# A fourth buffer for split weights, an early start of the state space stage's weights, and an early load of the square root's table

## The chip, the cores and the metric

The kernel runs on one core of a Trainium2 chip. The metric is the device time of one execution in microseconds (us), taken as the median of several executions. Engines are named as in the profile: PE multiplies matrices (TensorE), PEld loads its weights, DVE is VectorE, ACT is ScalarE, POOL is GpSimd, and SP issues most of the loads from memory.

## The reference, cut to what matters

One decoder layer is computed for 576 tokens, 512 of a prompt and 8 sequences of 8 sample tokens, with model width 1024, in float32:

```python
h = modulate(x, g_pre[0], shift0, scale0)
x = x + 0.5 * gate0 * rms_norm(swiglu(h, w_gate[0], w_up[0], w_down[0]), g_post[0])     # width 2816
h = modulate(x, g_pre[1], shift1, scale1)
q_lat, kv_lat, k_rope, z, xBC, dt, g_attn, g_ssm = split(h @ w_in)
o_attn = mla_attention(q_lat, kv_lat, k_rope) @ w_o_attn       # prompt, and samples over a paged cache
o_ssm  = mamba2(z, causal_conv(xBC), dt, state) @ w_o_ssm      # 4 groups of 8 heads, chunks of 128
mixed  = (sigmoid(g_attn) * o_attn + sigmoid(g_ssm) * o_ssm) @ w_out
x = x + gate1 * rms_norm(mixed, g_post[1])
h = modulate(x, g_pre[2], shift2, scale2)
x = x + 0.5 * gate2 * rms_norm(swiglu(h, w_gate[1], w_up[1], w_down[1]), g_post[2])
```

`rms_norm` divides by a root of the mean square; `modulate` is a norm with a scale and a shift from the sequence's vector. Outputs are x, the latent cache rows, and the new convolution and state space states.

## The kernel before, in words

Channels lie on the 128 partitions and tokens along the free dimension, in two halves of 288 tokens (`HALF`). Nearly every product is made three times in a reduced float32 format: each operand is split in a high part, `hi`, and a remainder, `lo`, and PE sums hi by hi, hi by lo and lo by hi. Activations are split where they are made. Weights are split when they arrive: `weights` (line 146) loads a 512 KB tile `wraw` on SP's queue, ACT copies it to `whi` (line 167), and DVE, or POOL for every second tile once `pool_weights` is set, subtracts to give `wlo` (line 113, called from line 168). The count that picks the engine, `wcount`, goes up by one with every call of `weights`. The pool `wp` holds three buffers each of `wraw`, `whi` and `wlo`. A pool `up` of 40 equal buffers of 608 floats per partition (`NU`) holds nearly everything else: activations, convolution rows, chunk matrices, states.

`gemm` splits a tile's weights and puts its product on a list, `pending`; a product is issued when more than `look[0]` are on that list. One tile of 8 by 128 input channels is 24 matmuls for one token half and 48 for both. `product` also runs the closures left on `later` after its matmuls and before its own evacuation. `flush` issues everything that is pending.

`Split` computes half 0 of all its tiles first, then half 1, so that the second half's input may come late. The split weights of its last `keep` tiles stay in `whi` and `wlo` for the second half, those of `far` more tiles stay in buffers of `up` (four of them for a tile), and the rest are loaded and split again.

The stages in order of time: the first feed-forward block, whose hidden width beyond the first six tiles goes through a seven-product block scheme (class `Wino`, lines 213 to 293: seven small weight blocks for each pair of tiles, two blocks in one `whi` buffer); its last down projection, merged with the normalisation of half 0 (`renew`); the first eleven tiles of `w_in` in a `Split` named `few` (gates, six convolution tiles of state space group 0, and the tile with dt); the state space stage; the latent and key/query tiles; attention of the prompt; attention of the samples; the two output projections; the second feed-forward block, which begins with another `Split`.

Outside of a block `with in_order():` a planner orders the instructions of each engine by its own estimate of times. Inside, PE, ACT, DVE and POOL run in the order in which the program is written. The state space stage is such a block: a generator `dense` issues the projections, a generator `scan` the chunks, and lines 1366 to 1378 interleave them. Before its first chunk the block calls `next(work)` `PRE` = 4 times, which splits four tiles of group 1 and issues two products. Ahead of it, lines 1005 to 1010 run the second half of `few`, call the three steps of `steps()` (time steps, sums, and a small product at line 979 that needs `last` from DVE at line 976), and `flush`.

`Sums` adds squares over tiles: `add` squares a tile on ACT (line 440), accumulates on POOL or DVE, and after the last tile a product with ones (line 430) sums over partitions. `rnorm` (line 451) takes the root on ACT and the reciprocal on DVE. The root needs another table of ACT than Silu, Tanh and Exp, and the compiler puts a table load ahead of the instruction that needs it.

Of the kernel before, what the change touches and what calls it, by code (L numbers as in the profile page):

```python
# [9 lines left out]
F32R = mybir.dt.float32r  # L10
BF16 = mybir.dt.bfloat16
I32 = mybir.dt.int32
AF = mybir.ActivationFunctionType
# [9 lines left out]
SCALE = 96 ** -0.5  # L23
NEG = -3.0e38
GAP = 603
NU = 40


def layer_kernel(tc, A, O, tap=None, stop=None):
# [7 lines left out]
def _layer(ctx, tc, A, O, tap, stop):  # L37
    nc = tc.nc
    V, S, PE, G = nc.vector, nc.scalar, nc.tensor, nc.gpsimd

    cp = ctx.enter_context(tc.tile_pool(name="cp", bufs=1))
    up = ctx.enter_context(tc.tile_pool(name="up", bufs=NU))
    wp = ctx.enter_context(tc.tile_pool(name="wp", bufs=3))
# [51 lines left out]
    def small(shape, dt=F32):  # L95
        return sp.tile(shape, dt, tag="small", name="small", bufs=24)
# [12 lines left out]
    def f32(ap):  # L109
        return ap.bitcast(F32)  # L110
# [18 lines left out]
    def in_order():  # L129

        E = mybir.EngineType
        return tc.manual_schedule(engines={E.PE, E.Activation, E.DVE, E.Pool})
# [15 lines left out]
    def weights(src, kc, far=False):  # L148

        out = []  # L150
        wcount[0] += 1
        pool = wcount[0] % 2 == 0 and pool_weights[0]
        for k0 in range(0, kc, 8):
            n = min(8, kc - k0)
            raw = wp.tile([128, 8, 128], F32, tag="wraw", name="wraw")
            if far:
                load(raw[:, :n], src[:, k0 * 128:(k0 + n) * 128].rearrange("p (k m) -> p k m", m=128))
                for k in range(0, n, 4):
                    hi, lo = (utile(F32R, [128, 4, 128], t) for t in ("fhi", "flo"))
                    S.copy(hi, raw[:, k:k + 4])  # L160
                    sub(lo, raw[:, k:k + 4], f32(hi), pool)
                    out += [(hi[:, j], lo[:, j]) for j in range(4)]
                continue
            hi = wp.tile([128, 8, 128], F32R, tag="whi", name="whi")
            lo = wp.tile([128, 8, 128], F32R, tag="wlo", name="wlo")
            load(raw[:, :n], src[:, k0 * 128:(k0 + n) * 128].rearrange("p (k m) -> p k m", m=128))
            S.copy(hi[:, :n], raw[:, :n])  # L167
            sub(lo[:, :n], raw[:, :n], f32(hi[:, :n]), pool)
            out += [(hi[:, j], lo[:, j]) for j in range(n)]
        return out  # L170
# [10 lines left out]
    look = [0]  # L181
# [33 lines left out]
    def flush():  # L215
        while pending:
            pending.pop(0)()
        settle()

    class Wino:  # L220
# [3 lines left out]
        def __init__(self, kc, x, area):  # L224

            self.kc, self.x, self.area, self.store = kc, x, area, None

        def block(self, src):

            kc = self.kc  # L230
            if self.store is None:
                self.store = [wp.tile([128, 2, 4, 128], F32R, tag=t, name=t) for t in ("whi", "wlo")]
                n = 0
            else:
                n = 1
            hi, lo = (t[:, n, :kc] for t in self.store)
            if n == 1:
                self.store = None
            S.copy(hi, src)  # L239
            sub(lo, src, f32(hi))  # L240
            return [(hi[:, j], lo[:, j]) for j in range(kc)]
# [56 lines left out]
    class Split:  # L298

        def __init__(self, tiles, kc, xh, xl, first=0, keep=2, then=None, far=0):
            self.tiles, self.kc, self.xh, self.xl, self.first, self.keep, self.then = tiles, kc, xh, xl, first, keep, then
            self.far = far

        def half0(self, first=True, last=True):
            if first:
                flush()
            kc, xh, xl, few = self.kc, self.xh, self.xl, self.first
            self.w = w = [weights(src, kc) for src, _ in self.tiles[:few]]  # L310
            if self.then:
                self.then()
            if few:
                ps = [mmt() for _ in range(few)]
                for k in range(kc):
                    for n in range(few):
                        mm3(ps[n][:, :HALF], *w[n][k], xh(k, 0), xl(k, 0), k == 0, k == kc - 1)
                for n in range(few):
                    self.tiles[n][1](0, 0, ps[n][:, :HALF])
            n0 = len(self.tiles) - self.keep  # L320
            for n, (src, evac) in enumerate(self.tiles[few:], few):
                w.append(weights(src, kc, n0 - self.far <= n < n0))
                gemm(None, kc, xh, xl, evac, (0,), w=w[-1])
                yield
            if last:
                flush()
# [92 lines left out]
    class Sums:  # L419
# [12 lines left out]
        def add(self, src, wait=False):  # L432
            self.k += 1
            last = self.k == self.n
            if self.acc is None:
                self.acc = s = utile(F32, [128, HALF], "acc")
                S.activation(s, src, AF.Square)
            else:
                s = tmp("sq")
                S.activation(s, src, AF.Square)  # L440
                (G if self.pool and not last else V).tensor_tensor(self.acc, self.acc, s, ALU.add)  # L441
            if last or self.k % self.group == 0:
                acc, self.acc = self.acc, None
                if wait:
                    later.append(lambda: self.square(acc, last))
                else:
                    self.square(acc, last)
# [143 lines left out]
    def ffn(n, xh, xl, side, last, wino, first=0, again=None):  # L591
# [39 lines left out]
        for part, (a, b) in enumerate(PARTS):  # L631
# [3 lines left out]
            tiles = []  # L635
# [36 lines left out]
            if part == 0:  # L672
                if again:
                    few = Split(tiles, 8, *parts(lambda k: (xhs[:, k], xls[:, k])), first, then=again[0])
                    yield few.half0()
                    merge((few.half1(), 1), (again[1], AGAIN))
                else:
                    few = Split(tiles, 8, *X, first)
# [12 lines left out]
            H = parts(lambda k, hs=hs: hs[k])  # L691
# [14 lines left out]
            tiles = [(A["w_dn"][n, m, :, 128 * a:128 * b], ev_down(m)) for m in range(NQ)]  # L706
            if part < end_:
                for src, ev in tiles:
                    if part:
                        product(src, b - a, *H, ev)  # L710
                    else:
                        gemm(src, b - a, *H, ev)
                        next(sums_, None)
            else:
                run(side)
                down = Split(tiles, b - a, *H, far=3)
                half0 = down.half0(first=False)
                next(half0)
                pending.insert(-1, settle)
                next(half0)  # L720
                wino.end()
                run(half0)
                merge((down.half1(), 1), (last(0, f, sums[0]), RENEW))
                yield last(1, f, sums[1])
# [9 lines left out]
    xT, _ = xtile(F32, "xT")  # L734
# [74 lines left out]
    xh, xl = X2s  # L809
# [184 lines left out]
    few = Split([gate(m) for m in next_gates(EARLY)] + c0[:5] + [(W[2], ev_kd), c0[5]], 8, *X2)  # L994
# [7 lines left out]
    done("x1")  # L1002
    pool_weights[0] = True
    st = steps()
    for n, _ in enumerate(few.half1()):
        if n in (2, 7):
            next(st, None)
    run(st)
    look[0] = 0
    flush()  # L1010

    def chunk_fetch(it):
        g, c = it["g"], it["c"]
# [281 lines left out]
    osm, _ = xtile(F32, "osm")  # L1295
# [15 lines left out]
    PRE = 4  # L1311
# [51 lines left out]
    work = dense()  # L1363
    age = 0
    credit = 1.0
    with in_order():
        look[0] = 2
        for _ in range(PRE):
            next(work)
        for _ in scan():  # L1370
            if kept:
                age += 1
                if age > 1:
                    put()
                    age = 0
            credit += RATE[min(len(closed), 3)]
            while credit >= 1:
                next(work, None)
                credit -= 1
        run(work)  # L1380
        flush()
        put()
        look[0] = 0
# [8 lines left out]
    for m in range(NQ):  # L1392
        ts = utile(F32, [128, T], "ts")
        load(ts, gscr[8 + m])
        for i in range(2):
            c = slice(i * HALF, i * HALF + HALF)
# [25 lines left out]
    def value_weights(p):  # L1422
        raw = wp.tile([128, 2, 256], F32, tag="wraw", name="wraw")
        if p == 0:
            wh, wl = (wp.tile([128, 2, 256], F32R, tag=t, name="wv") for t in ("whi", "wlo"))
        else:
            wh, wl = (vwp.tile([128, 2, 256], F32R, tag="wv", name="wv") for _ in range(2))
        load(raw, A["w_uv"][p // 2].rearrange("p (k b) -> p k b", k=2))
        S.copy(wh, raw)
        G.tensor_tensor(wl, raw, f32(wh), ALU.subtract)  # L1430
        wv_[p // 2] = wh, wl
# [352 lines left out]

    def split(it):

        it["c"] = hi, lo = [wp.tile([128, 4, 256], F32R, tag=t, name="c" + t) for t in ("whi", "wlo")]
        it["kp"] = kp = utile(F32R, [96, 4, 128], "kp")
        S.copy(hi[:, :, :128], it["raw"][:, :, 256:384])
        S.copy(kp, it["raw"][:96, :, 512:])  # L1790
# [167 lines left out]
    wv = []  # L1958
# [51 lines left out]
    xT, _ = xtile(F32, "xT2")  # L2010
# [169 lines left out]
```

## Time and profile before

| | us |
|---|---|
| median of 3 runs | 1990.33 (1987.17 to 1992.01) |
| the profiled execution | 1989.74 |
| its span, first to last instruction | 1988.0 |
| PE / DVE / ACT / POOL busy | 1889.4 / 1426.6 / 1023.5 / 628.2 |

The mean granted clock of PE in the span is 0.985 of full speed. The page gives 1368 matmuls of each of the three kinds for line 203's `xh`/`xl` products alone, at about 300 ns of overlapping duration each. In the rows below a `[x <-...]` at the end of a line is the time for which the engine sat idle before the instruction and what ended that.

### The profile page before, as it was taken

Reading aid. Unit: us, or ns where it says so; the run is one execution under the profiler, and the core shown is the slowest. Engines: PE = TensorE matmul, PEld = TensorE weight load, DVE = VectorE, ACT = ScalarE, POOL = GpSimd, SP = SyncE. Lnnn points to the kernel's source line nnn. Section 1 sums busy time; section 2 is a strip of 40 time slices with the busy share of each in tenths; the row PEclk is TensorE's granted clock in tenths of the full one; section 3 lists DMA queues with packets and bytes.
Section 4 is the critical chain, followed back from the end, with each engine's and each line's share of the span. In section 5 each row is a group of like instructions: output and inputs, shape, how many; then the busy total and the mean of one; then the engine's idle time right before and its main releaser. Section 6 shows DMA issues by size and latency. Waiting matters only on the chain.

```text
span 1988.0 us, 37032 instructions
## 1 busy us (share of the span) xinstructions
PE 1889.4 (95%) x13779; PEld 1746.5 (88%) x13779; DVE 1426.6 (72%) x2595; ACT 1023.5 (51%) x2237; POOL 628.2 (32%) x645
## 2 busy tenths in 40 slices
PE   6999999998989999999999899999989999999997
PEld 5999888998888999999899778776688999999997
DVE  4787575868776685667767677788956884866885
ACT  4655343556555465545434456566545664534553
POOL 1214234416343232332333111133332421422533
PEclk9999999999989999999999999999999999999998
DMA  9433545354554538454536444287857553232252
GB/s 322 138 117 122 188 136 170 98 172 131 183 130 147 160 105 221 127 177 149 165 108 210 136 165 138 89 272 265 288 181 244 164 171 99 83 97 87 94 168 77
DMA packets 171670, 312.79 MB, mean 157 GB/s; under 512 B 18097, under 2 KB 84370, under 8 KB 171490
## 3 DMA queue, kind: packets, MB, share of 16 engines
q1 hardware_dynamic: 145506, 267.93, 42.4%
q0 software_dynamic: 9088, 34.11, 4.9%
q10 hardware_dynamic: 16896, 8.39, 1.5%
q8 instruction: 108, 1.77, 0.4%
q14 instruction: 72, 0.59, 0.1%
HBM read 283.54 MB, written 26.83 MB: 156 GB/s over the span
## 4 chain that ended last, share of the span: by engine, by line
PE 44%; DVE 10%; ACT 3%; DMA 3%; issue 2%; POOL 1%; SPq 0%; DVEq 0%; ACTq 0%; POOLq 0%
PE mm L203 27%; PE mm L264 5%; DVE wlo L113 2%; PE mm L1576 2%; DMA wraw<-w_gu 1%; PE aux L1852 1%; DVE kp L113 1%; PE aux L1649 1%; DVE xbc L849 1%; PE mm L174 1%; ACT whi L167 1%; POOL cwlo L113 1%; PE mm L1631 1%; DVE small L1825 1%; PE mm L175 1%
## 5 line engine op out<-in xcount | busy, mean ns | idle before, releaser
L113 DVE TENSOR_TENSOR wlo<-wraw,whi 128x512 fp32r<-128x512 f32 (+2 forms) x296 | 320.9, 1086 | 126.9 <-ACT whi L167 86.5
L167 ACT CAST whi<-wraw 128x1024 fp32r<-128x1024 f32 (+2 forms) x260 | 234.2, 902 | 254.2 <-PE mm L203 146.1
L203 PE MATMUL mm<-xh,whi 128*128 128x288 f32 (+1 forms) x1368 | 346.2, 303 | 7.9 <-ACT xh L492 4.4
L203 PE MATMUL mm<-xl,whi 128*128 128x288 f32 (+1 forms) x1368 | 342.0, 300 | 4.1 <-DVE xl L482 3.2
L203 PE MATMUL mm<-xh,wlo 128*128 128x288 f32 (+1 forms) x1368 | 339.2, 298 | 6.6 <-POOL wlo L113 6.5
L203 PEld LDWEIGHTS mm<-xh,whi 128*128 128x128 f32 x1368 | 238.5, 192 | 16.0 <-ACT xh L492 4.6
L203 PEld LDWEIGHTS mm<-xh,wlo 128*128 128x128 f32 x1368 | 238.1, 191 | 7.6 <-POOL wlo L113 6.9
L203 PEld LDWEIGHTS mm<-xl,whi 128*128 128x128 f32 x1368 | 238.3, 191 | 5.7 <-DVE xl L482 3.9
L113 POOL TENSOR_TENSOR wlo<-wraw,whi 128x1024 fp32r<-128x1024 f32 (+1 forms) x60 | 122.6, 2044 | 166.4 <-ACT whi L167 159.3
L264 PE MATMUL mm<-t,whi 128*128 128x288 f32 x768 | 154.4, 295 | 1.3 <-DVE u L289 0.9
L264 PE MATMUL mm<-xh,wlo 128*128 128x288 f32 x512 | 150.1, 297 | 1.8 <-DVE wlo L113 1.8
L203 PE MATMUL mm<-hl,whi 128*128 128x288 f32 x608 | 151.5, 295 | 0.0
L264 PE MATMUL mm<-xl,whi 128*128 128x288 f32 x512 | 151.5, 297 | 0.0
L203 PE MATMUL mm<-hh,whi 128*128 128x288 f32 x608 | 151.2, 295 | 0.0
L264 PE MATMUL mm<-xh,whi 128*128 128x288 f32 x512 | 149.7, 297 | 0.0
L203 PE MATMUL mm<-hh,wlo 128*128 128x288 f32 x608 | 148.7, 296 | 0.3 <-DVE wlo L113 0.3
L113 DVE TENSOR_TENSOR wlo<-area,whi 128x512 fp32r<-128x512 f32 x128 | 116.4, 931 | 14.0 <-ACT whi L239 12.8
L264 PEld LDWEIGHTS mm<-t,whi 128*128 128x128 f32 x768 | 123.0, 188 | 3.2 <-issue 1.3
L264 PE MATMUL mm<-t,wlo 128*128 128x288 f32 x384 | 113.0, 296 | 1.7 <-DVE wlo L113 1.7
L441 POOL TENSOR_TENSOR acc<-acc,sq 128x288 f32<-128x288 f32 x72 | 71.5, 995 | 126.3 <-ACT sq L440 102.4
L203 PEld LDWEIGHTS mm<-hl,whi 128*128 128x128 f32 x608 | 104.9, 188 | 3.4 <-issue 3.4
L203 PEld LDWEIGHTS mm<-hh,whi 128*128 128x128 f32 x608 | 104.7, 188 | 3.5 <-ACT whi L167 1.7
(440 smaller groups left out, 4685.0 us busy)
## 6 DMA issues: line engine op xcount, KB each, us to landing
wraw<-w_gu SPq DMA_DIRECT2D x108, 512.0 KB, 3.5
craw<-cache SPq DMA_DIRECT2D x128, 320.0 KB, 4.4
wraw<-w_in SPq DMA_DIRECT2D x72, 512.0 KB, 4.0
wada<-w_ada SPq DMA_DIRECT2D x80, 256.0 KB, 4.6
area<-w_ada POOLq DMA_DIRECT2D x16, 1024.0 KB, 6.0
wraw<-w_dn SPq DMA_DIRECT2D x22, 512.0 KB, 4.7
wraw<-w_dn SPq DMA_DIRECT2D x32, 256.0 KB, 2.7
M<-cscr SPq DMA_DIRECT2D x32, 256.0 KB, 5.1
```

Of the source, the lines that this page charges most:

```text
L113: (G if pool else V).tensor_tensor(out, a, b, ALU.subtract)
L167: S.copy(hi[:, :n], raw[:, :n])
L174: PE.matmul(ps, ah, bl, start=False, stop=False, skip_group_check=skip)
L175: PE.matmul(ps, al, bh, start=False, stop=stop, skip_group_check=skip)
L203: PE.matmul(p[:, :m.shape[-1]], a, m, start=(k == 0 and n == 0), stop=(k == kc - 1 and n == 2))
L264: PE.matmul(ps, l, r, start=(start and j == 0 and n == 0), stop=(stop and j == self.kc - 1 and n == 2), skip_group_check=True)
L441: (G if self.pool and not last else V).tensor_tensor(self.acc, self.acc, s, ALU.add)
L849: V.scalar_tensor_tensor(a[:, 0:600], u[:, k:k + 600], cw[:, n, k:k + 1], a[:, 0:600], ALU.mult, ALU.add)
L1576: PE.matmul(pss[i][:, :HALF], a, x[k][:, i * HALF:i * HALF + HALF], start=(k == 0 and a is w[k][0] and x is qlh), stop=(k == 3 and a is w[ ...
L1631: PE.transpose(ps[:, c0 + 128 * (i - j):c0 + 128 * (i - j) + 128], block(p, e, i, j), ident)
L1649: PE.matmul(ps[64 * e:64 * e + 64, 128 * j:TP], vt[j // 2][:, j % 2, c0:c0 + 64], src, start=(j == 0), stop=(j == 3), tile_position=(0, 64 ...
L1825: V.tensor_reduce(mx[:, g:g + 1], ps, AX.X, ALU.max)
```

## The change

Four buffers of `whi` and `wlo` where there were three; `NU` goes from 40 to 37. The last down projection of each feed-forward block keeps two far tiles where it kept three. `few.half1` no longer flushes, and the flush after the steps is gone; two of the four calls of `next(work)` now come ahead of the ordered block. After the square of the last but one tile of a sum with `wait`, ACT takes the root of one column into a small tile that nobody reads. `Split` takes a parameter `spare`, which no caller passes.

```diff
-NU = 40
+NU = 37
@@ weights (also Wino.block, value_weights and the samples' split)
-            hi = wp.tile([128, 8, 128], F32R, tag="whi", name="whi")
-            lo = wp.tile([128, 8, 128], F32R, tag="wlo", name="wlo")
+            hi = wp.tile([128, 8, 128], F32R, tag="whi", name="whi", bufs=4)
+            lo = wp.tile([128, 8, 128], F32R, tag="wlo", name="wlo", bufs=4)
@@ Split.half0
-                w.append(weights(src, kc, n0 - self.far <= n < n0))
+                w.append(weights(src, kc, n0 - self.far <= n < n0 or n in self.spare))
@@ Sums.add
+            if wait and self.k == self.n - 1:
+                S.activation(small([128, 1]), s[:, 0:1], AF.Sqrt)
@@ ffn, last part
-                down = Split(tiles, b - a, *H, far=3)
+                down = Split(tiles, b - a, *H, far=2)
@@ second half of few
-    for n, _ in enumerate(few.half1()):
+    for n, _ in enumerate(few.half1(False)):
         if n in (2, 7):
             next(st, None)
     run(st)
-    look[0] = 0
-    flush()
@@ state space stage
+    look[0] = 2
+    for _ in range(2):
+        next(work)
     with in_order():
-        look[0] = 2
-        for _ in range(PRE):
+        for _ in range(PRE - 2):
             next(work)
```

## Rows read from the trace of the kernel before

**Rows 1.** The page's part 1: busy us, share of the span, instructions.
```profile
PE 1889.4 (95%) x13779; PEld 1746.5 (88%) x13779; DVE 1426.6 (72%) x2595; ACT 1023.5 (51%) x2237; POOL 628.2 (32%) x645
```
**Rows 2.** Busy time by stretch: PE, PEld, DVE, ACT, POOL, granted clock, DMA share, GB/s.
```profile
550.00:575.00 25.00, 18.11 (x115) 17.69 (x114) 17.68 (x19) 10.16 (x19) 11.97 (x17) 0.80 0.48 127
1650.00:1675.00 25.00, 25.00 (x190) 25.00 (x189) 12.99 (x25) 11.23 (x26) 0.98 (x1) 1.00 0.34 99
```
**Rows 3.** Waits of PE in the whole span: total us, times, longest.
```profile
PE mm L203 <- POOL wlo L113: 7.7, 3, 5.2
...
PE mm L203 <- ACT whi L167: 4.0, 5, 2.1
...
PE mm L264 <- DVE wlo L113: 3.5, 5, 1.4
...
PE mm L203 <- DVE wlo L113: 2.7, 4, 1.8
```
**Rows 4.** PE's timeline, 554.5 to 563 us: start, duration, instruction, idle before.
```profile
556.63 0.48 PE L979 MATMUL aux<-last,psel 32*128 32x128 f32 x2 [1.65 <-DVE last L976]
562.36 0.85 PE L203 MATMUL mm<-xh,wlo 128*128 128x288 f32 x2 [5.24 <-POOL wlo L113]
```
**Rows 5.** POOL's timeline, 555 to 567 us.
```profile
556.27 3.01 POOL L846 COPY ncvs<-u 128x24 f32<-128x24 f32 x1
...
559.43 2.87 POOL L113 TENSOR_TENSOR wlo<-wraw,whi 128x1024 fp32r<-128x1024 f32 x1
```
**Rows 6.** ACT's timeline, 547 to 571 us.
```profile
547.99 1.05 ACT L167 CAST whi<-wraw 128x1024 fp32r<-128x1024 f32 x1 [0.36 <-PE mm L203]
...
570.98 0.40 ACT L836 COPY u<-mm 128x288 f32<-128x288 f32 x1 [6.46 <-PE mm L203]
```
**Rows 7.** Busy time by stretch around the entry of the state space stage.
```profile
555.00:562.00 7.00, 0.48 (x2) 0.29 (x2) 6.96 (x8) 2.71 (x6) 6.21 (x5) 0.71 0.48 126
562.00:567.00 5.00, 4.64 (x19) 4.65 (x20) 3.88 (x3) 0.70 (x1) 4.09 (x6) 0.50 0.46 138
```
**Rows 8.** DVE's timeline, 441 to 470 and 555 to 573 us.
```profile
444.86 1.97 DVE L452 RECIPROCAL aux<-aux 128x288 f32<-128x288 f32 x1 [1.28 <-ACT aux L451]
...
556.50 1.21 DVE L113 TENSOR_TENSOR wlo<-wraw,whi 128x1024 fp32r<-128x1024 f32 x1
...
572.77 0.84 DVE L849 SCALAR_TENSOR_TENSOR xbc<-u,conv_w,xbc 128x600 f32<-128x600 f32 x1 [6.03 <-ACT xbc L847]
```
**Rows 9.** PE's timeline at three more waits.
```profile
469.19 1.09 PE L203 MATMUL mm<-xh,whi 128*128 128x288 f32 x3 [4.36 <-ACT xh L492]
...
1521.89 0.41 PE L203 MATMUL mm<-ahl,wlo 128*128 128x288 f32 x1 [1.82 <-DVE wlo L113]
...
1581.29 0.41 PE L203 MATMUL mm<-xh,whi 128*128 128x288 f32 x1 [2.12 <-ACT whi L167]
```
**Rows 10.** Busy time by stretch after the wait at 1581 us.
```profile
1582.00:1585.40 3.40, 3.40 (x16) 3.40 (x15) 3.40 (x5) 1.27 (x4) 1.54 (x2) 0.50 0.70 233
```
**Rows 11.** ACT's timeline around roots, and around the wait at 1581 us.
```profile
443.06 1.28 ACT L451 ACT_TABLE_LOAD   x1
444.35 0.47 ACT L451 ACTIVATE aux<-aux,eps_t 128x288 f32<-128x288 f32 x1
...
1514.39 0.47 ACT L451 ACTIVATE aux<-aux,eps_t 128x288 f32<-128x288 f32 x1 [1.37 <-PE aux L430]
...
1577.53 1.05 ACT L167 CAST whi<-wraw 128x1024 fp32r<-128x1024 f32 x1 [1.10 <-PE mm L203]
1578.60 1.28 ACT L642 ACT_TABLE_LOAD   x1
```
**Rows 12.** Waits in the state space stage, 575 to 1040 us: of SP, ACT, PE.
```profile
SPq L63 <- DMA o_ssm_s<-sn: 43.7, 11, 16.9
...
ACT whi L167 <- DMA o_ssm_s<-sn: 27.2, 3, 13.2
...
PE aux L1059 <- DVE H L1113: 3.1, 4, 1.9
```

More of the change, by code (lines that the diff above doesn't have):

```diff
@@ L231, in block @@
             if self.store is None:
-                self.store = [wp.tile([128, 2, 4, 128], F32R, tag=t, name=t) for t in ("whi", "wlo")]
+                self.store = [wp.tile([128, 2, 4, 128], F32R, tag=t, name=t, bufs=4) for t in ("whi", "wlo")]
                 n = 0
@@ L298, in _layer, with __init__ @@
     class Split:
-        def __init__(self, tiles, kc, xh, xl, first=0, keep=2, then=None, far=0):
+        def __init__(self, tiles, kc, xh, xl, first=0, keep=2, then=None, far=0, spare=()):
             self.tiles, self.kc, self.xh, self.xl, self.first, self.keep, self.then = tiles, kc, xh, xl, first, keep, then
-            self.far = far
+            self.far, self.spare = far, spare
         def half0(self, first=True, last=True):
@@ L1424, in value_weights @@
         if p == 0:
-            wh, wl = (wp.tile([128, 2, 256], F32R, tag=t, name="wv") for t in ("whi", "wlo"))
+            wh, wl = (wp.tile([128, 2, 256], F32R, tag=t, name="wv", bufs=4) for t in ("whi", "wlo"))
         else:
@@ L1785, in split @@
     def split(it):
-        it["c"] = hi, lo = [wp.tile([128, 4, 256], F32R, tag=t, name="c" + t) for t in ("whi", "wlo")]
+        it["c"] = hi, lo = [wp.tile([128, 4, 256], F32R, tag=t, name="c" + t, bufs=4) for t in ("whi", "wlo")]
         it["kp"] = kp = utile(F32R, [96, 4, 128], "kp")
```

## The prediction

> **What bounds the kernel now.** I read the page's busy shares first: PE is busy for 95% of the span [rows 1], and in a good stretch it issues 190 matmuls in 25.00 us at the full clock [rows 2], 0.132 us each. No other engine comes near that share. So the span shrinks only where PE stands still or runs at the lower of its two clock levels, and the second view is a table of stretches: it has one slice, 550 to 575 us, with 18.11 of 25.00 us busy and a granted clock of 0.80 [rows 2]. The third view is PE's list of waits. Its entries for split weights are short: 7.7 us on POOL's subtraction, 4.0 on ACT's cast, 3.5 and 2.7 on DVE's subtraction [rows 3], 17.9 together or 0.9% of the span. That is nearly all a fourth weight buffer can reach, apart from clock losses behind these waits.
>
> The bad slice is the entry of the state space stage. PE finishes the last tile of `few` just before 555, waits 1.65 us for `last` from DVE, does the small product of line 979, and waits 5.24 us for POOL's remainder of the first tile of group 1 [rows 4]. The clock is then 0.50 until about 567 [rows 7]: the first product starts at 562.36 and its evacuation at 570.98 [rows 4, 6], 8.62 us for 48 matmuls that take 48 x 0.132 = 6.3 at full clock, so 2.3 more are lost. The entry costs 1.65 + 5.24 + 2.3 = 9.2 us.
>
> Why is the remainder late? The cast to `whi` of that tile was done at 547.99 to 549.04 [rows 6], long before. POOL took it up at 559.43 [rows 5], because it first had line 846 for the last tile of `few`, a copy that ran to 559.28; the tile's own row preparation and subtraction stand in the ordered block behind it. A fourth buffer alone would not mend this; the order must.
>
> **The change part by part.** *The entry.* Two of the four `next(work)` move ahead of the block, and the last tile of `few` stays pending, so its 24 matmuls (3.2 us) run after these two tiles were put to the engines. Nothing is added: four tiles are split and two products issued before the first chunk, as before. What moves is two casts of 1.05 us, two subtractions, the row preparations on POOL, and two 512 KB loads, which SP may issue only in program order; the load that is moved ahead passes no chunk load, since these follow in `scan` either way. The far tile below adds one call of `weights` in the first block, which turns the alternation: the first tile's remainder falls to DVE (1.21 us [rows 8]) and not to POOL (2.87 [rows 5]). Behind the entry DVE has a backlog (6.96 of 7.00 us busy [rows 7]) but then idles 6.03 us until the first product is evacuated [rows 8]; so DVE can follow a PE that comes some 7 us earlier. The gain lies between 0 and 9.2. I take 7.0: the 5.24 and 2.3 go, less half a us of hand-over, and the wait for `last` stays, since DVE's backlog is what makes it late.
>
> *Four buffers at the second feed-forward block's start.* PE waits 2.12 us at 1581.29 for a cast [rows 9] that stands on ACT behind another cast, which waited for a buffer that PE held, and behind a table load of 1.28 us [rows 11]; then PE runs 3.40 us at 0.50 [rows 10], 1.7 lost. With four buffers both casts can stand ahead of the table load. Bounds 0 and 3.8; I take 2.5.
>
> *Four buffers elsewhere.* Of the 17.9 us of weight waits, 5.24 and 2.12 are counted above; 10.5 remain. The longest is 1.82 at 1521.89 [rows 9]; there a cast one tile earlier would also free `wraw` for its next load one tile earlier. In the state space stage no listed wait of PE is for weights at all (its longest entry is 3.1 us for a state from DVE [rows 12]), and in the ordered stages ACT evacuates the tile before it casts the next, so the fourth buffer is idle there. Bounds: 10.5 gained, or 2 lost where an earlier subtraction of 1.21 us steps ahead of a normalisation on DVE. I take 3.0 gained, a little under a third.
>
> *The root's table.* The load at 443.06 takes ACT 1.28 us, the root starts 0.01 later, and DVE's reciprocal had idled 1.28 for it [rows 11, 8]. That chain ends in PE's wait of 4.36 us at 469.19 [rows 9], so up to 1.28 us return. At 1514.39 ACT idled another 1.37 us for PE after its load [rows 11], so nothing returns; the sums whose table is already in place only add a one-column root on ACT, ten of them, each shorter than the 0.40 us of a 288-column copy [rows 6], beside PE's work. I take 1.0.
>
> By the Trainium skill ("ScalarE: Activation LUTs", section "What ACT_TABLE_LOAD costs") a switch is the load of about 1283 ns and about 1380 ns of drain, 2.66 us in all. The rows have the load alone, with no idle time on either side; by the page's figure this term would be up to 2.66 and the sum an estimated 1.4 us lower.
>
> *One far tile fewer.* The second half splits one more tile again in each of two blocks: a cast of 1.05, a subtraction of 1.21, a load. PE has three earlier tiles to work on meanwhile, and DVE shares the stretch with the normalisation of half 0; so 0 to 1.2 us each, I take 0.8 for both.
>
> *Three fewer slots in `up`.* SP waits 43.7 us in the state space stage for slots whose content is still being stored [rows 12]; with 37 slots these waits grow. Bounds 0 and the last rival's 25; I take 1.0, as the present waits reach ACT (27.2) but no listed wait of PE [rows 12]. The parameter `spare` is passed by nobody and costs nothing.
>
> Sum: -7.0 - 2.5 - 3.0 - 1.0 + 0.8 + 1.0 = -11.7. The profiled execution took 1989.74 us (span 1988.0 and 1.7 around it), 0.6 below the median of the runs, less than their spread; 1989.7 - 11.7 = **1978.0**.
>
> **The rivals.** *The entry wait changes its name.* POOL's copy of 24 columns took 3.01 us [rows 5] while DVE was busy throughout [rows 7]. Two subtractions put into that stretch may be as slow, or stand behind DVE's convolution steps, and PE waits as long as now. For it: DVE has no free time from 555 to 562. Against it: one subtraction needs 1.2 us, its cast was ready 13 us before use. Entry gain 0: 1989.7 - 4.7 = 1985. The Trainium skill ("SBUF — State Buffer", "SBUF: two separate sides") has DVE and GpSimd lock a shared port pair for a whole instruction, the other one blocked; the 3.01 us agrees with that, and by that rule this rival is likelier than the free DVE time after 567 suggests.
>
> *Fewer slots stall the load queue (slower).* SP's waits for slots average 43.7 / 11 = 4.0 us, and ACT stood up to 13.2 us behind them [rows 12]. Three slots fewer can mean three more such waits in a row, 12 us, at each of the three places where ACT already waited. PE is covered by two split tiles; it starts to lose once ACT's wait grows past the 13.2 that it hides today. If half of the 12 shows, 3 x 6 = 18 us, with a clock loss as at the entry each time (3 x 2.3 = 7): 1978 + 25 = 2003. Against it: the two down projections, where far tiles fill `up`, give four slots back each.
>
> *It doesn't do what it says.* Outside the ordered block the planner places the early weights by its own times; if it places them where they were, and its other shifts cancel: 1990.
>
> *All of it.* 9.2 + 3.8 + 10.5 + 1.3 = 24.8: 1965.
>
> **How the numbers follow.** The forecast has 0.53 (own range 1971 to 1984), the renamed entry wait 0.20, no effect 0.10, slots 0.10, all of it 0.07. The range 1968 to 1990 leaves out the slots, some of the no effect case and the tip of the last: under 2 in 10. A difference under 0.3% (6 us) can't be told from none here. Faster (below 1984.4): 0.51 of the forecast, 0.07, and half of the entry rival, 0.68 in all. Slower: the slots and a tip of no effect, 0.11. Same: 0.21.
>
> **What would show it.** Right: no PE wait over 2 us between 554 and 572, the clock at 1.00 there, the first subtraction of group 1 ended before the last `few` product; no 2.12 us wait and no 0.50 at the second block's start; a table load well before the root near 443, and PE's wait near 469 shorter. Wrong: PE waiting at the entry for DVE in POOL's place; SP's waits on stored states well above 43.7 us with PE waits on weights between 600 and 1040; new waits of PE in the feed-forward blocks, where the planner has reordered DVE.

## The result and the profile after

The changed kernel takes 1966.98 us (median of four runs, 1965.98 to 1972.4); the kernel before, beside it, 1990.3. The ratio is 0.989, with a 95% interval of 0.9868 to 0.9912: 23 us less. The forecast was 1978.0, so the direction was right and the size 11 us short; the time lies 1.0 below the range. The profiled execution of the changed kernel is the slowest of its four (1972.4, span 1970.6), so the two profiled executions differ by 17.3 us and not by 23. A second profile of the same kernel, taken with the experiments, has a span of 1967.7.

The page's busy times hardly moved against [rows 1]: PE has the same work, and only stands still or runs slow for less time.

```profile
PE 1888.8 (96%) x13779; PEld 1747.8 (89%) x13779; DVE 1433.0 (73%) x2595; ACT 1027.1 (52%) x2247; POOL 642.6 (33%) x645
```

The list of PE's waits over the whole span, against [rows 3]. POOL's remainder fell from 7.7 to 1.7, ACT's cast from 4.0 to 0.9, DVE's in the block scheme (line 264) from 3.5 to 1.5; DVE's for plain tiles grew from 2.7 to 3.7. Two entries are new or grown: `M`, the matrix of a chunk that DVE finishes at line 1076, with a wait of 2.7, and `osm`, the sum of the state space output that DVE adds to at line 1303.

```profile
PE mm L203 <- DVE wlo L113: 3.7, 5, 1.8
PE aux L1095 <- DVE M L1076: 3.4, 3, 2.7
...
PE mm L203 <- DVE osm L1303: 2.2, 1, 2.2
...
PE mm L203 <- POOL wlo L113: 1.7, 2, 1.2
...
PE mm L264 <- DVE wlo L113: 1.5, 2, 0.8
...
PE mm L203 <- ACT whi L167: 0.9, 2, 0.5
```

The stretches that answer to [rows 2] (the entry of the state space stage, now 540 to 565) and to [rows 10] (the start of the second feed-forward block): columns as there. Both are at the full clock, and PE is busy throughout.

```profile
540.00:565.00 25.00, 25.00 (x190) 24.71 (x189) 21.20 (x24) 14.89 (x32) 16.22 (x23) 1.00 0.51 139
...
1565.00:1575.00 10.00, 10.00 (x77) 10.00 (x76) 9.01 (x15) 7.95 (x14) 5.49 (x7) 1.00 0.67 231
```

To see where the time went, I cut every profile at four instructions that PE runs in each of these kernels (`rest` is made by DVE in the time steps, `xss` holds the sample tokens' rows): the first sum product behind the first feed-forward block (442.1 in the kernel before), the product with `rest` in the second half of `few` (541.1), the first transposes of the first chunk (577.3), and the first product with `xss` (638.1). Lengths of the five parts, in us of single profiled executions:

| kernel | to the sum product | to `rest` | entry | first chunks | all behind | span |
|---|---|---|---|---|---|---|
| before | 442.1 | 98.9 | 36.2 | 60.8 | 1349.9 | 1988.0 |
| changed | 431.3 | 96.1 | 29.4 | 64.0 | 1349.9 | 1970.6 |
| changed, second profile | 432.7 | 96.1 | 26.4 | 64.7 | 1347.8 | 1967.7 |
| early start alone | 441.0 | 98.3 | 26.6 | 62.8 | 1356.7 | 1985.3 |
| four buffers and their price | 431.7 | 95.9 | 30.0 | 60.0 | 1347.8 | 1965.5 |
| root's table alone | 441.6 | 98.3 | 35.8 | 60.7 | 1351.3 | 1987.9 |
| the price alone | 442.8 | 97.6 | 32.0 | 60.2 | 1347.5 | 1980.2 |
| alternation turned alone | 443.0 | 97.5 | 32.0 | 60.2 | 1346.8 | 1979.4 |
| changed, no early start | 430.7 | 95.5 | 31.6 | 60.0 | 1350.0 | 1967.9 |
| changed, no root | 432.5 | 96.7 | 26.4 | 63.1 | 1349.7 | 1968.3 |
| four buffers, turned back | 430.7 | 94.0 | 35.7 | 60.8 | 1349.7 | 1970.9 |
| changed, turned back | 431.6 | 94.4 | 26.2 | 60.8 | 1352.3 | 1965.2 |
| fourth raw buffer alone | 430.4 | 98.5 | 35.9 | 60.7 | 1356.1 | 1981.5 |
| both fourth buffers, 35 slots | 432.5 | 94.6 | 31.7 | 60.0 | 1348.7 | 1967.5 |

Nearly 11 of the 17 us are gained where the prediction saw little: in the first feed-forward block. The entry gains 7 to 10, and the first chunks give 3 to 4 of that back.

**The first feed-forward block.** These are three waits of the kernel before, from PE's timeline, and POOL's timeline ahead of the second:

```profile
267.25 0.40 PE L264 MATMUL mm<-t,wlo 128*128 128x288 f32 x1 [1.29 <-DVE wlo L113]
...
343.78 1.08 PE L388 MATMUL aux<-area,sq_c 128*32 128x512 f32 x4 [3.19 <-DMA area<-w_ada]
...
373.07 0.40 PE L264 MATMUL mm<-xh,wlo 128*128 128x288 f32 x1 [1.44 <-DVE wlo L113]
```

```profile
329.40 1.29 POOL L250 TENSOR_TENSOR area<-area,wraw 128x512 f32<-128x512 f32 x1 [5.27 <-DMA wraw<-w_gu]
...
335.27 0.77 POOL L75 DMA_DIRECT2D area<-w_ada  x1
```

The middle one is the largest, and no split weights are in it: PE waits for a load of `w_ada`, the weights of scales and shifts. POOL issues it between its sums of raw weight blocks, and those sums wait for raw tiles, 5.27 us of it just ahead of this load. In the changed kernel POOL issues the same load, the ninth of ten, at 325.93. Behind the wait the clock is at its lower level: the first line below shows it. The others are the whole stretch, before and then after:

```profile
343.78:349.85 6.07, 6.07 (x26) 4.41 (x27) 5.06 (x4) 2.27 (x5) 6.05 (x5) 0.51 0.13 19
...
225.00:440.00 215.00, 207.71 (x1512) 193.07 (x1512) 149.40 (x225) 96.98 (x196) 78.89 (x60) 0.98 0.46 153
```

```profile
225.00:440.00 215.00, 212.87 (x1586) 200.27 (x1585) 159.16 (x237) 103.57 (x206) 81.33 (x64) 1.00 0.49 159
```

In the same 215 us PE starts 1586 matmuls instead of 1512, and the granted clock is 1.00. 74 more matmuls at the 0.132 us of [rows 2] are 9.8 us, nearly all of the 10.8 in the table.

**The entry**, against [rows 4 to 8]. ACT's casts of the first two tiles of group 1, DVE's timeline, POOL's, and one later row of PE's:

```profile
533.35 1.05 ACT L167 CAST whi<-wraw 128x1024 fp32r<-128x1024 f32 x1 [0.65 <-PE mm L203]
...
537.13 1.05 ACT L167 CAST whi<-wraw 128x1024 fp32r<-128x1024 f32 x1 [0.99 <-PE mm L203]
```

```profile
534.43 1.23 DVE L113 TENSOR_TENSOR wlo<-wraw,whi 128x1024 fp32r<-128x1024 f32 x1 [1.21 <-ACT whi L167]
...
580.34 1.21 DVE L113 TENSOR_TENSOR wlo<-wraw,whi 128x1024 fp32r<-128x1024 f32 x1
581.47 1.28 DVE L1076 TENSOR_TENSOR M<-M,cbm 128x512 f32<-128x512 f32 x2
```

```profile
538.32 2.81 POOL L113 TENSOR_TENSOR wlo<-wraw,whi 128x1024 fp32r<-128x1024 f32 x1 [1.90 <-ACT whi L167]
...
543.83 7.02 POOL L834 COPY u<-cvs 128x24 f32<-128x24 f32 x1
550.78 0.10 POOL L833 MEMSET u<- 128x3 f32 x1
550.82 0.20 POOL L834 COPY u<-cvs 128x24 f32<-128x24 f32 x1
```

```profile
582.30 0.48 PE L1095 MATMUL aux<-M,xd 128*64 128x128 f32 x2 [2.69 <-DVE M L1076]
```

DVE makes the first tile's remainder at 534.43, right behind its cast, and POOL the second's at 538.32. Both are done before POOL runs into a copy of 24 columns that takes 7.02 us, a jam of the kind that held back the remainder in the kernel before. PE does not feel it any more. But 25 us later PE waits 2.69 us for `M`, which stands on DVE behind a subtraction: PE has come forward, DVE has not.

### The profile page after: what moved, and what is told of

Same layout as the page of the kernel before. It is cut to its first block, busy times and chain, and to the rows that moved or that the text cites. A ratio compares the mean times of both kernels' runs of the same rounds, so it can differ in the third digit from the quotient of the medians.

```text
span 1970.6 us, 37005 instructions
## 1 busy us (share of the span) xinstructions
PE 1888.8 (96%) x13779; PEld 1747.8 (89%) x13779; DVE 1433.0 (73%) x2595; ACT 1027.1 (52%) x2247; POOL 642.6 (33%) x645
## 5 line engine op out<-in xcount | busy, mean ns | idle before, releaser
L113 DVE TENSOR_TENSOR wlo<-wraw,whi 128x512 fp32r<-128x512 f32 (+2 forms) x300 | 336.9, 1126 | 124.7 <-ACT whi L167 94.8
L203 PE MATMUL mm<-hl,whi 128*128 128x288 f32 x640 | 161.2, 296 | 0.0
L203 PE MATMUL mm<-hh,whi 128*128 128x288 f32 x640 | 160.3, 295 | 0.0
L203 PE MATMUL mm<-hh,wlo 128*128 128x288 f32 x640 | 158.4, 295 | 0.0
L113 DVE TENSOR_TENSOR wlo<-area,whi 128x512 fp32r<-128x512 f32 x128 | 121.7, 965 | 12.2 <-ACT whi L239 11.6
L203 PEld LDWEIGHTS mm<-hl,whi 128*128 128x128 f32 x640 | 110.8, 188 | 3.5 <-issue 3.4
L203 PEld LDWEIGHTS mm<-hh,whi 128*128 128x128 f32 x640 | 110.6, 188 | 3.5 <-ACT whi L167 1.7
```

What stands on the lines that cost most here:

```text
L113: (G if pool else V).tensor_tensor(out, a, b, ALU.subtract)
L203: PE.matmul(p[:, :m.shape[-1]], a, m, start=(k == 0 and n == 0), stop=(k == kc - 1 and n == 2))
```

## The experiments

Times are medians in us; a ratio is to the kernel before on the same chip in the same minutes.

**The early start alone.** Edit on the kernel before:

```diff
-    for n, _ in enumerate(few.half1()):
+    for n, _ in enumerate(few.half1(False)):
...
-    look[0] = 0
-    flush()
...
+    look[0] = 2
+    for _ in range(2):
+        next(work)
     with in_order():
-        look[0] = 2
-        for _ in range(PRE):
+        for _ in range(PRE - 2):
```

> The kernel before with the early start alone (no flush behind few, two calls of next(work) ahead of the ordered block; 40 slots, three buffers, three far tiles). Theory, by the two traces: PE no longer waits for POOL's remainder of the first tile of group 1, the clock stays at its upper level from 555 to 567, and the state space stage begins some 10 us earlier (9.2 worked out from before, 10.2 read from after): 1980 to 1982. Rival: the early start works only with the fourth buffer, because with three the second early tile must wait for a tile that PE still holds; then the wait of 5.2 us becomes one of 2 to 4 us and the time is 1985 to 1988. Rival two: the gain at the entry is given back in the chunks behind it, by waits of PE for DVE: 1988 to 1991.

Measured: 1987.45 against 1992.48, ratio 0.9973 (0.9962 to 0.9984), 5 us faster, where 1980 to 1982 was expected. The entry is mended with three buffers too (36.2 to 26.6), so the first rival falls by its mechanism, though the time is the one that it gave. Of these 9.6 us the first chunks take back 2.0 by waits for DVE, which is part of the second rival. The rest of the kernel takes back 6.8 in this profile. Some of that is the clock: a wait of nearly the same length, at the same place, was followed by the full clock in the kernel before (first fence) and by the lower level here (second fence). The 64 small matmuls of line 2003 took 2.09 and 3.62 us, 1.5 us of difference.

```profile
1482.63 0.40 PE L203 MATMUL mm<-mhl,whi 128*128 128x288 f32 x1 [1.30 <-ACT mhl L1927]
...
1483.58 2.09 PE L2003 MATMUL aux<-olat,wv 128*64 128x64 f32 x64
1483.00:1486.40 3.40, 3.31 (x73) 3.05 (x73) 0.36 (x2) 2.82 (x5) 2.37 (x1) 1.00 0.43 142
```

```profile
1475.84 0.40 PE L203 MATMUL mm<-mhl,whi 128*128 128x288 f32 x1 [1.35 <-ACT mhl L1927]
...
1476.80 3.62 PE L2003 MATMUL aux<-olat,wv 128*64 128x64 f32 x64
1476.90:1480.30 3.40, 3.40 (x64) 3.33 (x64) 0.98 (x1) 2.32 (x4) 2.27 (x1) 0.50 0.22 55
```

**Four buffers and what pays for them.** Edit: `bufs=4` on all tiles of `whi` and `wlo`, `NU = 37`, `far=2`.

> The kernel before with the fourth buffer of whi and wlo alone, and what pays for it (37 slots, two far tiles). Theory, by the two traces: PE comes to the end of the first feed-forward block's wide part some 10 us earlier, since the waits for wlo there go and with them the wait of 3.2 us for the w_ada load at 343.8 and the lower clock behind it, and the wait of 2.1 us at the second block's start goes: 1976 to 1980. The prediction's terms for these parts (-2.5, -3.0, +0.8, +1.0) give 1986.6. Rival: the first block's gain does not come from the buffer but from the planner, which places steps differently in every program: then anywhere from 1985 to 1993, with the waits at 343.8 and 373 still there.

Measured: 1965.71, ratio 0.9859 (0.9845 to 0.9874), 27 us faster by the medians and 28 by the ratio: as fast as the whole change, and 10 us below the range expected. The first block gains 10.4 and has no wait over 0.8 us between 225 and 440. The surprise is the entry: without any early start it falls from 36.2 to 30.0, with a wait of 1.90 us in place of 1.65 and 5.24:

```profile
551.75 0.40 PE L203 MATMUL mm<-xh,wlo 128*128 128x288 f32 x1 [1.90 <-POOL wlo L113]
```

**The root's table alone.** Edit on the kernel before:

```diff
+            if wait and self.k == self.n - 1:
+                S.activation(small([128, 1]), s[:, 0:1], AF.Sqrt)
```

> The kernel before with the root's table alone. Theory: nothing that can be measured, 1989 to 1991, because in the trace of after PE's wait ahead of the first tile of few is 4.36 us as before. The prediction's term of -1.0 would give 1989.3 and a wait of 3.1 to 3.4 us there. Rival: the added roots of one column change the planner's order, and the time moves by 3 us or more in either direction with waits of PE at places where no root stands.

Measured: 1991.89, ratio 0.9998 (0.9989 to 1.0007). Nothing, and no part of the table moved by more than 1.4 us.

**The price alone.** Edit on the kernel before: `NU = 37` and `far=2`.

> The kernel before with only what pays for the fourth buffer: 37 slots and two far tiles, three buffers. By the prediction (+0.8 and +1.0) 1992.1. If fewer slots stall the load queue, 1997 or more, with PE waits for weights between 600 and 1040. If the gain in the first feed-forward block comes from these numbers, not from the buffer, 1980 to 1984 with the waits at 343.8 and 373 gone.

Measured: 1982.77, ratio 0.9947 (0.9933 to 0.9961): 10 us faster by what I had priced at 1.8 slower. The gain is not in the first block (442.8 to the sum product, with a wait of 3.4 us for the `w_ada` load) but in the entry, 4.2, and "all behind", 2.4, which none of the three cases had in mind.

**The alternation turned alone.** One far tile fewer is one more call of `weights`, and each call turns the engine for the subtraction. Edit on the kernel before, nothing else:

```diff
     pool_weights[0] = True
+    wcount[0] += 1
     st = steps()
```

> The kernel before with nothing but the alternation turned from the second half of few on (the count goes up by one where POOL begins to share the subtractions), so DVE makes the remainder of the first tile of group 1 and POOL that of the second. Theory: this alone explains what 37 slots and two far tiles gave (-10 us): at the entry PE works on the first tile while DVE makes last, and waits 3.5 us for POOL's remainder of the second instead of 1.65 and 5.24, a gain of 4 to 6 us there; and 3 to 4 us near 910, where the waits for sn go: -7 to -11 in all. Rival: the slots or the far tile gave it; then within 3 us of before.

Measured: 1984.71 against 1992.62, ratio 0.9964 (0.9953 to 0.9976), 8 us faster by the medians and 7 by the ratio. Its parts are those of the price alone within 0.7 us, so the turn carries most of that gain; the two ratios, 0.9964 and 0.9947, have intervals that overlap, and up to a few us may belong to the slots or the tile. POOL is stuck in a 24-column copy as ever, but the remainder behind it is the second tile's, and PE has the first tile to work on meanwhile (POOL's row, then PE's):

```profile
555.97 5.25 POOL L846 COPY ncvs<-u 128x24 f32<-128x24 f32 x1
```

```profile
565.00 0.45 PE L203 MATMUL mm<-xh,wlo 128*128 128x288 f32 x1 [3.50 <-POOL wlo L113]
```

**The changed kernel once more, without the early start, and without the root.** Three kernels on one chip: the changed kernel, and two in which one part of it is undone (the edits above, backwards; the unused `spare` is left out too).

> The changed kernel itself, once more, beside the variants of it, so that differences of 3 us between them can be told. Against the kernel before: -21 to -26 us (1967 to 1970 where before takes 1991). In its profile I expect the wait of some 2.7 us for M from DVE near 582 with a low clock behind it, which the kernel with four buffers alone does not have; if that wait is not there again, it is no cost of the early start.

> The changed kernel without the early start (the flush is back, all four calls of next(work) in the ordered block). Theory: with the fourth buffer, and with the alternation turned so that DVE makes the remainder of the first tile of group 1, the entry is already mended, and the early start adds nothing or costs: PE waits some 1.9 us for POOL's remainder of the second tile at the entry, but not for M near 582. So 1 to 4 us faster than the changed kernel. Rival, the prediction's step: the early start is what takes the entry's 7 to 9 us; then 7 us slower than the changed kernel.

> The changed kernel without the early load of the root's table. Theory: equal to it within 2 us, as on the kernel before, where the early load alone changed nothing (ratio 0.9998). The prediction's term says 1.0 us slower. Rival: the added roots changed the planner's order behind the state space stage (the changed kernel waits 2.2 us near 1043 for osm and is 5 us behind the kernel with four buffers alone); then 2 to 5 us faster.

Measured: changed 1967.01, ratio 0.9872 (0.9853 to 0.9892); no early start 1964.93, 0.9854 (0.9831 to 0.9876); no root 1970.11, 0.9877 (0.9857 to 0.9897). The root is worth nothing here either. Nor is the early start, in this company. Two stretches show it, in the changed kernel (first fence) and without the early start (second): at the entry PE has 1.91 us more work done, and between 575 and 600 it loses 3.08 more. The wait for `M` near 582 is there again, 3.2 us in this profile; without the early start no wait for `M` between 575 and 620 is over 0.3.

```profile
540.00:565.00 25.00, 25.00 (x189) 24.71 (x188) 21.20 (x27) 14.71 (x33) 15.27 (x22) 1.00 0.58 138
575.00:600.00 25.00, 21.41 (x155) 19.77 (x155) 19.45 (x34) 15.84 (x37) 7.47 (x9) 0.93 0.37 105
```

```profile
540.00:565.00 25.00, 23.09 (x162) 22.57 (x161) 19.05 (x24) 14.17 (x32) 14.64 (x18) 0.93 0.50 127
575.00:600.00 25.00, 24.49 (x197) 22.94 (x196) 20.75 (x35) 15.75 (x37) 6.34 (x10) 1.00 0.43 121
```

**Turned back.** The line `wcount[0] += 1` on four buffers with their price, and on the changed kernel: POOL gets the first tile's remainder again, as in the kernel before.

> Four buffers, 37 slots, two far tiles and no early start, with the alternation turned back from the second half of few on, so that POOL makes the remainder of the first tile of group 1 as in the kernel before. Theory: the turn is worth 7 us on the kernel before (ratio 0.9964) and does the same here, so this kernel loses 4 to 8 us against four buffers with the favourable alternation (0.9859): ratio to before 0.989 to 0.991, with PE's wait of 4 to 6 us for POOL at the entry. Rival: with the fourth buffer POOL makes that remainder earlier, before its slow copies, and the turn is worth nothing: 0.985 to 0.987.

> The changed kernel with the alternation turned back in the same way. Theory: the early start makes the entry independent of which engine gets the first tile, so here it is worth what it was meant to: no wait over 2 us at the entry, and 3 to 6 us faster than four buffers turned back without it (ratio to before 0.985 to 0.988). Rival: DVE's later wait for M near 582 takes it back here too: equal to the kernel without the early start within 2 us (0.989 to 0.991).

Measured on one chip: 1974.61, ratio 0.9915 (0.989 to 0.994), and 1970.97, 0.9901 (0.9876 to 0.9925). Without the early start the entry is as bad as ever (first fence), and the gain of four buffers is down from 27 us to 17. With it there is no wait at all (second fence), and the first chunks give nothing back: the first wait for `M`, near 582 in the changed kernel, is gone. Behind the product with `rest` and ahead of that place DVE makes three subtractions here, and four in the changed kernel and in the early start alone, which both wait; that this is the cause is not shown. In the profiles the early start brings 9.5 us at the entry; in the timed runs only 3.6 are left, with intervals that overlap, so they don't decide between theory and rival.

```profile
546.50 0.61 PE L203 MATMUL mm<-xh,wlo 128*128 128x288 f32 x1 [6.75 <-POOL wlo L113]
```

```profile
530.00:555.00 25.00, 25.00 (x190) 24.71 (x189) 22.23 (x26) 15.29 (x31) 22.06 (x25) 1.00 0.46 115
```

**A fourth raw buffer alone, and both.** Edits: `bufs=4` on `wraw`, on the kernel before with `NU = 38`; and on four buffers with `NU = 35`.

> The kernel before with a fourth buffer for the raw tiles wraw alone, and 38 slots for its room; split weights keep three buffers, the alternation is as before. It tells what frees PE in the first feed-forward block. Theory: the split buffers do, since a cast there waits for PE to let a buffer go, so raw tiles that come earlier change little: 0 to -3 us, with the waits for wlo at 267 and 373 and the 3.2 us for the w_ada load at 344 as before. Rival: the loads were the bound, a raw tile was let go too late and POOL's sums and its w_ada load stood behind it: then PE reaches 442 some 8 to 10 us earlier, as with the fourth split buffer, and the kernel is 8 to 10 us faster.

> Four buffers of raw and of split tiles, two far tiles, 35 slots, no early start. Theory: five slots fewer than before still stall nothing that PE waits for, and the raw buffer adds little to the split ones: 0.984 to 0.987, as four buffers with 37 slots. The prediction's rival of slots: SP's waits for slots grow and PE waits for weights in the state space stage: 0.99 or more. If raw tiles were the bound as well: 0.980 to 0.983, the fastest version.

Measured: raw alone 1983.07, ratio 0.9962 (0.9945 to 0.9978), 8 us faster; both 1969.18, ratio 0.9893 (0.9867 to 0.9918), slower than the 0.984 to 0.987 expected and not faster than the changed kernel. My theory of the raw buffer fell. With three split buffers and four raw ones PE has no wait at all in the first block, and the gain there is 11.7 us, as large as with the fourth split buffer:

```profile
225.00:440.00 215.00, 215.00 (x1603) 202.63 (x1602) 146.48 (x238) 104.45 (x207) 80.31 (x63) 1.00 0.48 155
```

So the bound there was the flow of raw tiles. POOL's waits for them between 225 and 440 add up to 64.5 us before, 53.0 in the changed kernel and 18.8 with the raw buffer. By the program a raw tile is let go when its cast and its sums are done, so a fourth split buffer, which lets the cast run sooner, should let the next load start sooner as well; this part is argued, not shown. A rival is that the planner, which orders every program anew, moved the load by chance. Against it stand all profiles together: PE's longest wait for a `w_ada` load in that stretch is 3.1 to 3.5 us in the five with three buffers of both kinds, and 0 to 2.3 in the nine with a fourth of either. The 2.3 is the kernel with both, and it gains 9.6 us in the first block. The raw buffer also shows that such a gain need not last: behind 638 its kernel loses some 6 of it. With 35 slots no wait of PE between 600 and 1040 is over 0.8 us, and none is for weights.

## Why the prediction was right in its direction and 11 us short

**Four buffers elsewhere: this step failed** (-3.0, bounds -10.5 and +2). Four split buffers measure 17 us on top of the price alone (1982.77 to 1965.71), where this term and that of the second block's start gave 5.5 together. The first block alone gained 9.4 to 11.4 in the profiles with four split buffers, and the stretch up to `rest` 2.2 to 4.9 more (the turned alternation alone gave 1.4 there). I took the reach of the fourth buffer from the list of waits *for split weights*, 10.5 us. The runs showed what that list leaves out. The largest wait that vanished is booked on a `w_ada` load, on another queue, held up because POOL's sums, ahead of it in POOL's order, waited for raw tiles. And the lower clock behind it, 6.07 us at 0.51, costs some 3 us (6.07 x 0.49) that no list of waits shows. The third view of the prediction had room for both: a wait for a DMA should have been followed to what its issuing engine waited for. By the Trainium skill ("DMA: Bandwidth & Descriptors", "Issuing engines are not separate DMA queues") loads of all engines run on the same 16 DMA engines and interleave. The trace agrees: this load was issued at 335.27, SP's loads of weights followed from 335.94, and 8.5 us passed until PE's product, against a median of 5.9 for the five loads of `w_ada` between 300 and 350. With 5.9 it would have landed at 341.2, 0.6 us after PE came to it, so the slow landing has a part in the wait beside the late issue.

**One far tile and three slots fewer: this step failed too, in its sign** (+0.8 and +1.0). Measured together: 10 us faster. The prediction had the cause in its hands: it says that the far tile turns the alternation and gives the first remainder to DVE. It used that only beside the early start, as a detail of the entry, and priced the tile by its instructions. The turn alone is worth 7 to 8 us.

**The entry** (-7.0, bounds 0 and 9.2). In the entry itself 6.8 went in the changed kernel's profile, 9.8 in the second, 9.6 with the early start alone; what the prediction listed as its signs all came: no wait over 2 us, the clock at 1.00, the first subtraction done before `few` ended. Two things make it worth less than that. The chunks behind it are paced by DVE: the prediction said that DVE could follow a PE some 7 us earlier, and it could not, so 3.2 to 3.9 came back near 582. And the turned alternation had already mended half of the entry by itself (36.2 to 32.0), so the prediction's "the order must" holds only with POOL on the first remainder. Beside it and the fourth buffer, the early start measures as nothing (0.9854 without, 0.9872 with); alone, it is worth 5 us. So the terms of the sum were not independent.

**The second block's start** (-2.5, bounds 0 and 3.8). The wait and the low clock are gone, so the size held. The account did not quite: the prediction had both casts stand ahead of the table load, and ACT's order is the same as in [rows 11], a cast, the load, and the next casts behind it (last fence). But PE had other tiles to work on and did not wait for the cast behind the load. Between the two sum products around the place (before in the first fence, after in the second) PE starts 17 matmuls more in 1.73 us less, 1.73 + 17 x 0.132 = 4.0 us gained. Some is given back at once, as PE then waits 1.35 us for `xl`, where it waited 0.78 before: from this table load (1578.60 before, 1564.74 after) to the same later Silu (1618.70 and 1602.04), 2.8 remain.

```profile
1575.27:1593.94 18.67, 16.55 (x112) 16.15 (x111) 15.71 (x19) 11.61 (x19) 8.39 (x10) 0.91 0.57 193
```

```profile
1561.41:1578.35 16.94, 16.94 (x129) 16.83 (x128) 14.57 (x19) 11.51 (x18) 7.70 (x9) 1.00 0.57 207
```

```profile
1563.67 1.05 ACT L167 CAST whi<-wraw 128x1024 fp32r<-128x1024 f32 x1 [1.11 <-PE mm L203]
1564.74 1.28 ACT L644 ACT_TABLE_LOAD   x1
...
1566.34 1.99 ACT L167 CAST whi<-wraw 128x1024 fp32r<-128x1024 f32 x2
```

**The root's table** (-1.0, bounds 0 and 1.28). It loads early as forecast, at 425.18, and its root follows at 432.08 with no other table load between. But PE's wait near 469 is 4.36 us still, at 458.41. ACT's row shows why: the prediction had the wrong root in the chain that ends there. It is the next one, at 453.04, whose table was already in place and which waits for PE's own sum product.

```profile
425.18 1.28 ACT L443 ACT_TABLE_LOAD   x1
...
432.08 0.46 ACT L453 ACTIVATE aux<-aux,eps_t 128x288 f32<-128x288 f32 x1
...
453.04 0.47 ACT L453 ACTIVATE aux<-aux,eps_t 128x288 f32<-128x288 f32 x1 [1.68 <-PE aux L430]
```

**The rivals.** The entry wait did not change its name: the remainders were made ahead of the stretch in which DVE and POOL block each other. Slots did not stall the load queue: SP's waits for stored states in the state space stage fell to 38.2 us from the 43.7 of [rows 12], and 35 slots were harmless too. "All of it" (1965) was the nearest case, at 0.07 the least of all, and right by its number, not by its account: it gave the 10.5 us to waits for split weights. That the time came near it is luck.

What stays open: why the gains of the raw buffer and of the early start shrink by 6 to 7 us behind 638. The larger part is not waits. For the same 9296 matmuls PE is busy 3.9 us longer with the early start alone and 4.5 with the raw buffer (rows below: before, early start, raw buffer), so it ran slower; two of the stretches at the lower clock are that of the early start from 1476.90, above, and one from 1050.20 to 1053.70 with the raw buffer, at 0.51. The other 2.8 and 1.6 us are idle time of PE. Why the clock falls more often there, a single profile of each can't say.

```profile
638.05:1988.00 1349.95, 1293.80 (x9296) 1186.20 (x9293) 974.54 (x1888) 700.78 (x1587) 406.26 (x412) 0.99 0.49 157
...
628.65:1985.30 1356.65, 1297.65 (x9296) 1190.26 (x9293) 975.26 (x1888) 703.19 (x1587) 405.60 (x412) 0.99 0.50 156
...
625.46:1981.50 1356.04, 1298.31 (x9296) 1190.60 (x9293) 963.35 (x1888) 703.87 (x1587) 403.63 (x412) 0.99 0.49 156
```

## What to carry to other kernels

When a buffer is added, don't bound its gain by the waits for that buffer: follow each wait for a load back through the queue that issued it, and add the clock lost behind the wait. Check whether an edit changes a count that hands out work in turn; here one call more was worth 7 to 8 us, more than the planned early start (5 us alone). And when two parts of a change mend the same wait, their gains don't add: time each alone and each left out.

## What the runs showed of the hardware

The same copy of 24 columns on POOL took 7.02 us at 543.83 and 0.20 at 550.82 in the changed kernel, and the next instructions start 6.95 and 0.14 us later, so the span is real. During the long one DVE was busy for 6.58 of 7.00 us:

```profile
545.00:552.00 7.00, 7.00 (x53) 6.71 (x52) 6.58 (x9) 1.75 (x5) 7.00 (x7) 1.00 0.63 181
```

By the Trainium skill ("SBUF — State Buffer", "SBUF: two separate sides") the two engines share a port pair that one of them holds for a whole instruction while the other blocks, where DVE reads two inputs from SBUF and POOL reads SBUF too. The trace agrees the other way round: in the kernel before, while POOL made a remainder from 559.43 to 562.30 [rows 5], a step of DVE took 2.91 us, and the same line took 0.78 at 554.76.

```profile
560.03 2.91 DVE L853 SCALAR_TENSOR_TENSOR xbc<-u,xbc 128x600 f32<-128x600 f32 x1
```

For POOL it goes further: the long copy lasted through a chain of nine DVE instructions of 0.8 us each, and not through one alone. That is why work on POOL next to a busy DVE can't be priced by its usual duration.
